# Out-projection by seven products over all eight token tiles, with its right blocks and those of FFN pair 1 prepared in stage one through GpSimd's DMA queue

## The chip, the cores and the metric

One core of a Trainium2 chip runs the whole layer. The time is that of the device in microseconds, the median of several executions of the same program. TensorE (PE in the profile, with PEld for its weight loads) multiplies. VectorE (DVE), ScalarE (ACT) and GpSimd (POOL) work on tiles in the on-chip memory SBUF and on the results in PSUM. SyncE (SP) issues DMAs in the kernel before; in the changed one GpSimd issues some too.

## The reference

One layer of a streaming encoder, on 1024 tokens of width 1024 in float32. What bears on the change is the end of the mixer and the start of the FFN:

```python
h = x @ w_in[l]
...
y_a = chunk_band_attention(heads_a(qa), heads_a(ka), heads_a(va), rel_bias[l]) @ w_proj_a[l]
y_b = stick_breaking_attention(heads_b(qb), heads_b(kb), heads_b(vb)) @ w_proj_b[l]
gate_a = jax.nn.sigmoid(ga + b_gate[l, :D])
gate_b = jax.nn.sigmoid(gb + b_gate[l, D:])
mix = (gate_a * y_a + gate_b * y_b) @ w_out[l]
x = layer_norm(DEEPNORM_ALPHA * x + mix, ln1_g[l], ln1_b[l])
gu = x @ w_ffn_in[l]
g, u = jnp.split(gu, 2, axis=-1)
ffn = (jax.nn.silu(g) * u) @ w_ffn_out[l]
x = layer_norm(DEEPNORM_ALPHA * x + ffn, ln2_g[l], ln2_b[l])
```

## The kernel before

**Numbers in two parts.** A float32 operand is split (`split`, lines 108 to 110) into a high part, a rounded copy that ScalarE casts, and a low part, which VectorE subtracts. A product of two operands is three matmuls of 128x128 by 128x512: high by high, high by low, low by high. All three add into one PSUM bank.

**Seven products.** Where a matrix product is cut into 2 x 2 blocks, seven block products of sums and differences take the place of eight (a scheme of Strassen's kind). The products have numbers 1 to 7 and run in an order such as 1, 2, 5, 3, 6, 7, 4. Two PSUM banks per tile suffice: `x`, on which products 1, 6, 7 and 4 build, and `y`, with 2 and 3 or 5 and others. The sums are made ahead, by VectorE.

**Stages.** Stage one is the input projection. Its columns are taken in pairs of blocks (`project`, `pair_steps`), each by seven products, and after the products p1, p2, p6, p5, p7, p3, p4 of a pair the PSUM banks (`sxp`, `syp`, `szp` in the profile) are copied or added into tiles `c`, which then go to DRAM (`q_dr`, `k_dr`, `g_dr`). Beside this main work stage one does side work, called from `aside_work` (line 500): `sum_wo` loads blocks of the out-projection's weights, forms four differences and stores them raw in `wt_dr`; `store_proj` loads 8 blocks of the attention's projection weights, splits them and stores both parts in `wp_dr`. Side tiles and `c` tiles share the slots of `QKV`, that is of the tags `qs`, `kh`, `kl` and `v`, with two slots each. `cycle` hands them out in turn, and who gets a slot waits until its former tile has been read for the last time, by a store for example. Every DMA is issued on SP's queue (`dma = nc.sync.dma_start`).

Then come attention with its stick-breaking part, the projection of its result, the gates, and the out-projection.

**The out-projection before** (lines 1355 to 1420) treats the token tiles 0 to 3 by seven products over two tiles at a time, and the token tiles 4 to 7 in full: eight block products each, for two halves of the columns. The seven products read `wt_drt` (stage one's differences), loaded and split on the spot by `begin_wo`. `take_in` adds a finished bank into the residual tile `acc`. `norm_1` is LayerNorm 1: statistics, aggregate, a power on POOL, and two scalings by VectorE (`L1188` and `L1191`). As soon as four token tiles are normed, `x1_operands` transposes them on TensorE (`x1ps`), copies and splits them into the FFN's operands `x1A`.

**The FFN** takes the 22 column blocks of its input weights as 11 pairs. Pair 0 is computed in full (`plain_half`, tiles `plainhl` and `plainhr`), since its operands are not summed yet. Pairs 1 to 10 go by seven products. For each, `left_f` and `right_f` load the weights `wLf` and `wRf` and form and split the sums `taf`, `tbf`. For pair 1 this happens during the out-projection.

**Order.** The tile framework's scheduler orders each engine's instructions from the program's order, and `tc.keep_in_program_order` or `tc.issue_after` pin some. An engine works its own list in order: a waiting instruction holds up all behind it, DMA issues in a queue included.

```python
QKV = ("qs", "kh", "kl", "v")
SLOTS = dict(bw=9, pt=4, yt=3, qs=2, kh=2, kl=2, v=2, gt=3, kp=4, op=8, xt=16)
```

Of the kernel before, what the change touches and what calls it, by code (L numbers as in the profile page):

```python
# [18 lines left out]
P = 128  # L19
# [29 lines left out]
def hybrid_trunk_kernel(ctx: ExitStack, tc, x, xt, w_first, w_v, w_in, b_gate, rel_bias, w_proj,  # L49
# [117 lines left out]
    def product(acc, W, ops, p, first):  # L167

        if p == 3:
# [367 lines left out]
    def begin_w(srcs, name, raw, hl, lo_eng, in_turn=False):  # L537
        r = raw(f"wr_{name}")
        srcs = srcs if isinstance(srcs, list) else [(slice(0, 1024), srcs)]
        for cs, src in srcs:  # L540
            ins = dma(r[:, cs], src)
            if in_turn:
                tc.keep_in_program_order(ins)
# [23 lines left out]
    wt_dr = {n: dram(f"wt_dr{n}_", 2) for n in ("t1", "t2", "t3", "t4")}  # L567
    wo_src = {n: [w_out[b, j] for j in range(2)] for b, n in enumerate(("11", "12", "21", "22"))}

    def sum_wo(j):  # L570

        put, sub = nc.vector.tensor_tensor, ALU.subtract
        x_, y_, z_, u_ = (cycle(QKV, f"wo{n}r{j}") for n in ("11", "12", "21", "22"))
        for t, n in ((x_, "11"), (y_, "12"), (u_, "22"), (z_, "21")):
            dma(t, wo_src[n][j])
        put(x_, y_, x_, sub)
        put(y_, u_, y_, sub)
        put(u_, u_, x_, sub)
        put(z_, z_, u_, sub)
        for t, n in ((x_, "t1"), (y_, "t3"), (u_, "t2"), (z_, "t4")):  # L580
            dma(wt_dr[n][j], t)
# [3 lines left out]
    def store_proj(i):  # L585
# [4 lines left out]
        for d, t in zip(wp_dr[i], load_w(srcs, f"proj{i}", take, take, nc.vector)):  # L590
            dma(d, t.bitcast(F32))
# [70 lines left out]
    def right_or_v(i):  # L662
# [3 lines left out]
        else:  # L666
# [4 lines left out]
              right_or_v, first=3, then=rest_of_start, also=aside_work, wide=V_AT - 1, then_right=2)  # L671
# [325 lines left out]
    wo = {}  # L997

    def begin_wo(name, raws, tag):
        ends = [begin_w((wt_dr if name in wt_dr else wo_src)[name][j], f"o{name}_{j}", of(raw),  # L1000
                        of(tag), nc.vector, True) for j, raw in enumerate(raws)]

        def end():
            wo[name] = [end_j(True) for end_j in ends]
        return end

    def wo_op(name, kt):
        cs = (LO, HI)[kt % 2]
        return tuple(t[:, cs] for t in wo[name][kt // 2])

# [9 lines left out]
    for si, (hd, g, st, box) in enumerate(vsteps):  # L1020
# [5 lines left out]
        if pos == 4:  # L1026
            if hidx < 15:
                load_v(heads[hidx + 1])
            else:
                next_w = begin_proj(1, 3)()  # L1030
                end_11, end_21 = (begin_wo(name, raws, "xt")
                                  for name, raws in (("11", ("qs", "kh")), ("21", ("kl", "v"))))
        if hidx == 15 and pos == 10:
            end_11()
# [49 lines left out]
    m_high = [None] * 8  # L1084
    raw_22 = slot("pt", "m22")
    m_first = [slot(tag, f"m1_{kt}", F32R) for kt, tag in enumerate(("yt", "yt", "yt", "pt"))]
    m_ab = [[None] * 4 for _ in range(2)]
    acc_t = []

    def quarter(q):  # L1090
        return slice(q * 2 * P, (q + 1) * 2 * P)

    def m_sums(kt, a, b):

        put, sub = nc.vector.tensor_tensor, ALU.subtract
        g, (q0, q1, q2, q3) = m_first[kt], (quarter(q) for q in range(4))
        split(g[:, q2], g[:, q3], b[:, q0])
        nc.scalar.copy(raw_22[:, quarter(kt)], b[:, q1])
        put(b[:, q1], a[:, q1], b[:, q1], ALU.add)
        put(a[:, q1], a[:, q0], a[:, q1], sub)  # L1100
        put(a[:, q0], b[:, q1], a[:, q0], sub)
        put(b[:, q0], b[:, q0], a[:, q0], sub)
        for n, t in enumerate((a, b)):
            o = m_ab[n][kt] = slot("bw", f"m{'ab'[n]}_{kt}", F32R)
            split(o[:, LO], o[:, HI], t[:, LO])
# [6 lines left out]
    def m_op(p, kt):  # L1112
        if p in (1, 2):
            q = 0 if p == 1 else 2
            return m_first[kt][:, quarter(q)], m_first[kt][:, quarter(q + 1)]
        if p == 4:
            return tuple(t[:, quarter(kt)] for t in ops_22)
        o, q = {6: (m_ab[0], 0), 7: (m_ab[0], 1), 3: (m_ab[1], 0), 5: (m_ab[1], 1)}[p]
        return o[kt][:, quarter(q)], o[kt][:, quarter(q + 2)]

    m_raw = {}

    def high(c):
        t = m_high[c] = cycle(QKV, f"mo{c}", F32R)
        split(t[:, LO], t[:, HI], m_raw[c][:, HI])

    for n, c in enumerate((6, 7, 5, 4, 2, 3, 1, 0)):
        if n % 2 == 0:
            w = next_w
            if n < 6:  # L1130
                next_w = begin_proj(1, (2, 1, 0)[n // 2])()
# [16 lines left out]
        if c < 4:  # L1148
            m_sums(c, m_raw[c + 4], mA)
            if n > 4:  # L1150
                high(last_c)
            last_c = c
        else:
            g = m_first[c - 4]
            split(g[:, quarter(0)], g[:, quarter(1)], mA[:, quarter(0)])
            high(c)
        if n == 0:
            end_21()
        elif n == 3:
            more_acc("pt")  # L1160
            more_acc("pt")
        elif n == 6:
            end_t2 = begin_wo("t2", ("gt", "gt"), "op")
    end_t2()
    end_t1 = begin_wo("t1", ("gt", "bw"), "op")
    end_t3 = begin_wo("t3", ("gt", "gt"), "op")
    ops_22 = [slot("xt", f"m22{q}", F32R) for q in "hl"]
    split(*ops_22, raw_22)
    more_acc("pt")
# [6 lines left out]
    def layer_norm(t, g, b, name, quick, done=lambda cs: None, n_st=2, cuts=(LO, HI),  # L1176
                   late_low=False):
        st = sml.tile([P, 24], F32, name=f"bn_{name}", tag="bn")
        mv = sml.tile([P, 3], F32, name=f"mv_{name}", tag="mv")
        w = D // n_st  # L1180
        for j in range(n_st):
            at = (j + late_low * n_st // 2) % n_st * w
            nc.vector.bn_stats(st[:, 6 * j:6 * j + 6], t[:, at:at + w])
            if j == 0:
                nc.vector.tensor_scalar(st[:, 2:3], st[:, 2:3], EPS * D, None, ALU.add)
        nc.vector.bn_aggr(mv[:, 0:2], st[:, 0:6 * n_st])
        nc.gpsimd.tensor_tensor(mv[:, 2:3], mv[:, 1:2], neghalf, ALU.pow)
        nc.vector.scalar_tensor_tensor(t, t, mv[:, 0:1], g, ALU.subtract, ALU.mult)  # L1188
        if quick:
            for cs in cuts:  # L1190
                nc.vector.scalar_tensor_tensor(t[:, cs], t[:, cs], mv[:, 2:3], b[:, cs],  # L1191
                                               ALU.mult, ALU.add)
                done(cs)
        else:
            nc.scalar.activation(t, t, AF.Copy, scale=mv[:, 2:3])
            nc.gpsimd.tensor_tensor(t, t, b, ALU.add)
# [442 lines left out]
```

## Time and profile before

| | before |
|---|---|
| median of 3 runs | 1412.49 us (1411.85 to 1413.65) |
| the profiled execution | 1412.51 us |
| its span in the trace | 1410.7 us |
| instructions on TensorE | 6642 matmuls and transposes |
| bytes moved by DMA | 292.28 MB, 207 GB/s on average |
| granted clock of TensorE | 0.999 |

The span runs from the first to the last instruction that the trace shows; 1.8 us of the execution lie around it. Matmuls are pipelined: a 128x512 matmul is shown with a length of 0.39 us, and the next starts before it ends, so the spacing of starts tells its cost. Lines in the profile are those of the kernel before. A split has the lines 109 (ScalarE) and 110 (VectorE), and most products of stage one and the FFN line 179, so groups are told apart by tile names. On the timeline stage one lies between 0 and 315 us, attention with the gates and projections from there to about 640, the out-projection from 681.5 to 766.5, and the FFN behind it.

### The profile page before, as it was taken

Reading aid. Unit: us, or ns where it says so; the run is one execution under the profiler, and the core shown is the slowest. Engines: PE = TensorE matmul, PEld = TensorE weight load, DVE = VectorE, ACT = ScalarE, POOL = GpSimd, SP = SyncE. Lnnn points to the kernel's source line nnn. Section 1 sums busy time; section 2 is a strip of 40 time slices with the busy share of each in tenths; the row PEclk is TensorE's granted clock in tenths of the full one; section 3 lists DMA queues with packets and bytes.
Section 4 is the critical chain, followed back from the end, with each engine's and each line's share of the span. In section 5 each row is a group of like instructions: output and inputs, shape, how many; then the busy total and the mean of one; then the engine's idle time right before and its main releaser. Section 6 shows DMA issues by size and latency. Waiting matters only on the chain.

```text
span 1410.7 us, 18935 instructions
## 1 busy us (share of the span) xinstructions
PE 1399.7 (99%) x6642; PEld 1164.6 (83%) x6642; DVE 1034.1 (73%) x1671; ACT 699.0 (50%) x1245; POOL 236.0 (17%) x308
## 2 busy tenths in 40 slices
PE   9999999999999999999999999999999999999997
PEld 7888888888888888888888888888888888888886
DVE  8967657545887788878998967767677765847666
ACT  6544444545888888774413644434444443322220
POOL 0000000002555878750001000000000000000033
PEclk9999999999999999999999999999999999999999
DMA  7476468856676478755651144433444349996652
GB/s 254 165 286 224 178 236 303 295 179 238 212 231 208 130 252 281 253 198 194 231 202 75 61 148 166 149 141 143 164 164 149 143 144 342 411 385 236 233 194 90
DMA packets 98927, 292.28 MB, mean 207 GB/s; under 512 B 9728, under 2 KB 26112, under 8 KB 98832
## 3 DMA queue, kind: packets, MB, share of 16 engines
q1 hardware_dynamic: 98832, 291.07, 58.2%
q8 instruction: 52, 0.85, 0.3%
q14 instruction: 43, 0.35, 0.1%
HBM read 187.20 MB, written 100.17 MB: 204 GB/s over the span
## 4 chain that ended last, share of the span: by engine, by line
PE 94%; DVE 2%; DMA 1%; ACT 1%; issue 1%; POOL 0%; DVEq 0%; SPq 0%; ACTq 0%; POOLq 0%
PE sxf L179 16%; PE d L1512 15%; PE sxp L179 9%; PE szf L179 8%; PE v L481 5%; PE gps L606 4%; PE szp L179 4%; PE syf L179 4%; PE yAps L910 3%; PE ops L1369 3%; PE syp L179 2%; PE tp_b L817 2%; PE tp_a L817 2%; PE plain L347 1%; PE pv_b L833 1%; PE pv_b L832 1%
## 5 line engine op out<-in xcount | busy, mean ns | idle before, releaser
L1512 PE MATMUL d<-wd,sl 128*128 128x512 f32 (+1 forms) x924 | 207.7, 387 | 0.0
L1512 PEld LDWEIGHTS d<-wd,sl 128*128 128x128 f32 x924 | 172.3, 188 | 35.4
L1532 POOL TENSOR_TENSOR mv<-mv,neghalf 128x1 f32<-128x1 f32 x8 | 9.0, 1121 | 606.7 <-DVE mv L1531 606.7
L109 ACT CAST wd<-wd 128x512 fp32r<-128x512 f32 x77 | 45.9, 621 | 114.1 <-PE d L1512 66.8
L794 POOL TENSOR_TENSOR w_b<-w_b,kp_b 128x511 f32<-128x511 f32 (+3 forms) x96 | 96.0, 1012 | 23.2 <-DVE kp_b L789 16.7
L110 DVE TENSOR_TENSOR sl<-h,sl 128x512 fp32r<-128x512 f32 x77 | 52.6, 686 | 27.6 <-ACT sl L109 27.6
L789 DVE TENSOR_TENSOR_SCAN kp_b<-kp_b,ident_ps 128x512 f32<-128x512 f32 (+2 forms) x64 | 56.5, 885 | 21.0 <-ACT kp_b L786 20.0
L109 ACT CAST sl<-h 128x512 fp32r<-128x512 f32 x77 | 47.5, 620 | 48.1 <-PE syf L179 18.3
L1489 DVE TENSOR_TENSOR x<-d,x 128x512 f32<-128x512 f32 (+1 forms) x41 | 27.6, 675 | 47.6 <-PE d L1512 47.5
L786 ACT ACTIVATE kp_b<-sc_b 128x512 f32<-128x512 f32 (+3 forms) x96 | 48.3, 504 | 28.0 <-PE sc_b L706 23.6
L110 DVE TENSOR_TENSOR wd<-wd,wd 128x512 fp32r<-128x512 f32 x77 | 52.7, 709 | 10.7 <-ACT wd L109 10.6
L179 PE MATMUL szf<-x1S63h,wcf 128*128 128x512 f32 x168 | 55.1, 389 | 0.0
L110 DVE TENSOR_TENSOR pt_b<-tp_b,pt_b 128x512 fp32r<-128x512 f32 (+1 forms) x96 | 49.9, 544 | 6.6 <-ACT pt_b L109 5.7
L729 POOL MEMSET bias<- 64x64 f32 x2 | 0.3, 145 | 314.3 <-ACT bias L725 314.3
L109 ACT CAST pt_b<-tp_b 128x512 fp32r<-128x512 f32 (+1 forms) x96 | 46.6, 503 | 8.0 <-PE tp_b L817 7.6
L759 POOL TENSOR_SCALAR w_a<-w_a,st_a 128x640 f32<-128x640 f32 (+2 forms) x64 | 42.2, 669 | 48.0 <-PE sc_a L706 26.6
L754 ACT ACTIVATE w_a<-w_a,st_a 128x640 f32<-128x640 f32 (+2 forms) x64 | 44.7, 700 | 8.6 <-DVE st_a L748 7.5
L787 ACT ACTIVATE w_b<-sc_b 128x511 f32<-128x511 f32 (+3 forms) x96 | 48.3, 504 | 0.0
L817 PE MATMUL tp_b<-ident,w_b 128*128 128x128 f32 x288 | 47.3, 272 | 0.2
L110 DVE TENSOR_TENSOR pt_a<-tp_a,pt_a 128x512 fp32r<-128x512 f32 (+1 forms) x96 | 44.6, 486 | 3.3 <-ACT pt_a L109 2.2
L1307 ACT ACTIVATE h<-sxf 128x512 f32<-128x512 f32 x21 | 12.6, 598 | 68.2 <-PE sxf L179 68.2
L817 PEld LDWEIGHTS tp_b<-ident,w_b 128*128 128x128 f32 x288 | 36.4, 140 | 11.1 <-DVE pt_b L110 1.1
(1574 smaller groups left out, 4285.2 us busy)
## 6 DMA issues: line engine op xcount, KB each, us to landing
s_dr<-sl SPq DMA_DIRECT2D x77, 512.0 KB, 2.6
sl<-s_dr SPq DMA_DIRECT2D x77, 512.0 KB, 7.6
wLf<-in_w_ffn_in_dram SPq DMA_DIRECT2D x22, 512.0 KB, 4.3
wRf<-in_w_ffn_in_dram SPq DMA_DIRECT2D x22, 512.0 KB, 3.6
wd<-in_w_ffn_out_dram SPq DMA_DIRECT2D x22, 512.0 KB, 8.2
v_dr<-vc SPq DMA_DIRECT2D x16, 512.0 KB, 3.4
qs<-q_dr SPq DMA_DIRECT2D x16, 512.0 KB, 6.7
kh<-k_dr SPq DMA_DIRECT2D x16, 512.0 KB, 6.5
```

The source lines that it names most:

```text
L109: return (nc.scalar.copy(dst_h, src), nc.vector.tensor_tensor(dst_l, src, dst_h.bitcast(F32), ALU.subtract))
L110: nc.vector.tensor_tensor(dst_l, src, dst_h.bitcast(F32), ALU.subtract))
L179: mm(acc, lw[:, ks], rx, start=(first and kt == i == 0), stop=(kt == 3 and i == 2), skip_group_check=not first)
L481: mm(accs[j], a, b, start=(first and kt == n == 0), stop=(kt == 3 and n == 2), skip_group_check=True)
L606: mm(acc[hf], lw[:, ks], rx[k][:, (LO, HI)[hf]], start=(k == j == 0), stop=(k == KT - 1 and j == 2))
L754: nc.scalar.activation(s[:, 0:w], s[:, 0:w], AF.Exp, bias=st[:, m:m + 1], scale=-1.0, accum_out=st[:, 2:3])
L786: nc.scalar.activation(kp[:, c0:e], sc[:, 0:n], AF.Sigmoid, scale=-1.0)
L787: nc.scalar.activation(be[:, m0:e], sc[:, m0 - c0:n], AF.Sigmoid)
L789: nc.vector.tensor_tensor_scan(kp[:, 0:e], kp[:, 0:e], ident_ps()[:, 0:e], 0.0, ALU.mult, ALU.add)
L794: nc.gpsimd.tensor_tensor(be[:, m0:e], be[:, m0:e], kp[:, m0 - 1:e - 1], ALU.mult)
L817: ins = tr(tp[:, (qb - lo_q) * P:(qb - lo_q + 1) * P], wt[qb - q0][:, (kb - qb) * P:(kb - qb + 1) * P], ident)
L1512: mm(part, a, b, start=(fresh and i == k == 0), stop=(i == n - 1 and k == 2), skip_group_check=not fresh)
```

## The change

1. The out-projection goes by seven products over all eight token tiles: product p runs over four tile positions j, so that positions j and j + 4 are the two token blocks. The order is 1, 2, 5, 3, 6, then 7 and 4 interleaved. The left-hand operands of products 3 to 7 are split one by one between the products (`m_split`, `m_sums`, `m_sums_3`).
2. Of the out-projection's right blocks, 1, 2, 3 and 5 are loaded raw and split on the spot (`wo_split`), and 4, 6 and 7 are split in stage one, stored in `wo_dr` and loaded ready for use. The block of product 5 is a difference that stage one stores raw (`t1_dr`).
3. FFN pair 1's seven right blocks are summed and split in stage one too (`sum_wf`), stored in `wf_dr`, and loaded by `load_f1`.
4. The side transfers of stage one (these, and those of `store_proj`) are issued from GpSimd's queue: `aside_dma = nc.gpsimd.dma_start`. The tables `WO_AT` and `PROJ_AT` say at which pair of stage one which side work starts, and `next_part` runs one part of it after each product.
5. LayerNorm 1 scales the second time on VectorE only for the token tiles 3, 6 and 7. For 0, 1, 2, 4 and 5 ScalarE scales, and a DMA on GpSimd's queue adds the bias `ln1b` in place (`accum_op`). LayerNorm 1 and 2 share `mark` and `finish` now, and VectorE's order around the out-projection is tied by `chain`.

```diff
+    WO_AT, PROJ_AT = (5, 7, 8, 9, 10), (6, 9, 10, 11)
     def aside_work(i):
         if i == 2:
             small_inputs()
-        if i in (2, 6):
-            sum_wo(i // 6)
-        if i >= len(work) - 9:
-            store_proj(i - len(work) + 9)
+        if i in PROJ_AT:
+            for j in range(2):
+                store_proj(2 * PROJ_AT.index(i) + j)
+        if i + 1 in WO_AT:
+            parts.extend((sum_wf, *(lambda kt=kt: sum_wo(kt) for kt in range(4)))
+                         [WO_AT.index(i + 1)]())
...
+    aside_dma = nc.gpsimd.dma_start
+    def sum_blocks(name, x_, y_, z_, u_, dst):
+        sub, put = ALU.subtract, nc.vector.tensor_tensor
+        def out(p, src, *terms):
+            def part():
+                if terms:
+                    put(src, *terms, sub)
+                if p in dst:
+                    o = cycle(("kl", "v"), f"{name}_{p}", F32R)
+                    split(o[:, LO], o[:, HI], src)
+                    aside_dma(dst[p], o.bitcast(F32))
+                elif p == 5:
+                    aside_dma(dst["t1"], src)
+            return part
+        return [out(3, u_), out(1, x_), out(5, x_, y_, x_), out(7, y_, u_, y_),
+                out(6, u_, u_, x_), out(2, z_), out(4, z_, z_, u_)]
...
+    def finish(name, n, t, g, b, lone, done, cuts=(slice(0, D),), tied=False, added=None):
...
+        nc.gpsimd.tensor_tensor(mv[:, 2:3], mv[:, 1:2], neghalf, ALU.pow)
+        for cs in cuts:
+            tie(nc.vector.scalar_tensor_tensor(t[:, cs], t[:, cs], mv[:, 0:1], g[:, cs],
+                                               ALU.subtract, ALU.mult))
+            if lone:
+                tie(nc.vector.scalar_tensor_tensor(t[:, cs], t[:, cs], mv[:, 2:3], b[:, cs],
+                                                   ALU.mult, ALU.add))
+            else:
+                nc.scalar.activation(t[:, cs], t[:, cs], AF.Copy, scale=mv[:, 2:3])
+                if added is None:
+                    nc.gpsimd.tensor_tensor(t[:, cs], t[:, cs], b[:, cs], ALU.add)
+                else:
+                    nc.gpsimd.dma_start(t[:, cs], added[:, cs], accum_op=ALU.add)
...
+    def norm_1(tt):
+        finish(f"1_{tt}", 2, acc_t[tt], g1, b1, tt == 3 or tt > 5, lambda cs: None, tied=True, added=b1)
+    def project_out(p, j):
+        accs = by if p in (2, 5, 3) else bx
+        first = p in (1, 2, 5)
...
+        for kt in range(4):
+            lh, ll = (m_ops[p][kt][:, c + j * P:c + (j + 1) * P] for c in (0, HW))
+            wh, wl = (wo[p][kt][:, cs] for cs in (LO, HI))
+            for n, (a, b) in enumerate(((lh, wh), (lh, wl), (ll, wh))):
+                mm(accs[j], a, b, start=(first and kt == n == 0), stop=(kt == 3 and n == 2),
+                   skip_group_check=not first)
+        tt, cs = j + 4 * (p in (5, 7, 4)), (LO, HI)[p in (5, 7, 3, 6)]
+        take_in(tt, cs, accs[j], 1.0 if p in (2, 6, 7) else ALPHA)
...
+    for n, (p, j) in enumerate(((7, 0), (7, 1), (4, 0), (7, 2), (4, 1), (7, 3), (4, 2), (4, 3))):
+        project_out(p, j)
+        if p == 4:
+            norm_1(j + 4)
+        if n > 3:
+            x1_operands(0, acc_t, (n - 4,))
```

Three places where the change moves instructions. The first is ScalarE in stage one, between the pairs 8 and 9 (numbers behind the tile names: `c1_8` is the first `c` tile of pair 8, `sxp8` its bank). Before:

```order
L401 COPY c1_7_1700<-sxp7_1687 128x512
L386 ACTIVATE hi1_7_1813<-c1_7_1700 128x1024
L109 CAST wbp9h_1865<-tbp9_1861 128x1024
L198 COPY c1_8_1856<-sxp8_1843 128x512
L207 COPY c2_8_1909<-sxp8_1843 128x512
```

After, the same engine one pair later, from the last copy of pair 8 to the first of pair 9:

```order
L403 COPY c1_8_1879<-sxp8_1866 128x512
L109 CAST wo0_4_1961<-wo0b_1863 128x512
L388 ACTIVATE hi1_8_2009<-c1_8_1879 128x1024
L109 CAST wcp10_2049<-wRp10_2033 128x512
L109 CAST wbp10h_2040<-tbp10_2036 128x1024
L200 COPY c1_9_2031<-sxp9_2018 128x512
```

A cast of a block of the out-projection's weights (`wo0_4`) now stands between the copies of two pairs, and its tile takes a slot of the same ring as the `c` tiles.

The second is POOL in stage one. Before, POOL's list has nothing between setting up its constants and attention; after, it holds 65 DMAs there, of which these are some (`DMA a<-b` writes a; `wo0b` and `wo1a` are raw weights, `t1_dr` and `wo_dr` the stores):

```order
L605 DMA wo0b_1863<-in_w_out_dram 128x1024
L596 DMA t1_dr0_269<-wo0a_1862 128x512
L594 DMA wo_dr7_0_277<-wo0_7_1923 128x1024
L605 DMA wo1a_2014<-in_w_out_dram 128x1024
L594 DMA wo_dr6_0_273<-wo0_6_1942 128x1024
L594 DMA wo_dr4_0_281<-wo0_4_1961 128x1024
L605 DMA wo1b_2015<-in_w_out_dram 128x1024
```

Loads and stores share one queue, so a store that waits for its split also holds up the load behind it.

The third is VectorE at the out-projection's end. The tiles `acc` are residual tiles by token tile, and `ops1_0` is a PSUM bank, which product 7 of tile 0 leaves and product 4 of tile 0 then writes. After:

```order
L1388 SCALAR_TENSOR_TENSOR acc3_7281<-acc3_7281,ops1_3_7398 128x512
L1216 BN_STATS bn1_3_7674<-acc3_7281 128x6
L1224 BN_AGGR mv1_3_7782<-bn1_3_7674 128x2
L1227 SCALAR_TENSOR_TENSOR acc3_7281<-acc3_7281,mv1_3_7782,ln1g_7332 128x1024
L1230 SCALAR_TENSOR_TENSOR acc3_7281<-acc3_7281,mv1_3_7782,ln1b_7334 128x1024
L1388 SCALAR_TENSOR_TENSOR acc4_7418<-acc4_7418,ops1_0_7336 128x512
```

And TensorE there, in groups of three matmuls, from product 7 of tile 3 to the first transposes:

```order
L1405 MATMUL ops1_3_7398<-wo7_0_7596,m7_0_7710 128x512 x3
L1405 MATMUL ops1_3_7398<-wo7_1_7597,m7_1_7713 128x512 x2
L1405 MATMUL ops1_0_7336<-wo4_0_7688,m4_0_7350 128x512 x3
L1405 MATMUL ops1_0_7336<-wo4_1_7689,m4_1_7320 128x512 x3
L1405 MATMUL ops1_0_7336<-wo4_2_7690,m4_2_7222 128x512 x3
L1405 MATMUL ops1_0_7336<-wo4_3_7691,m4_3_7267 128x512 x3
```

Before, each of these token tiles had a bank of its own per half of the columns; after, product 4 comes into a bank that VectorE must have emptied, behind the whole LayerNorm 1 of token tile 3.

More of the change, by code (lines that the diff above doesn't have):

```diff
@@ L540, in begin_w @@
         for cs, src in srcs:
-            ins = dma(r[:, cs], src)
+            ins = load(r[:, cs], src)
             if in_turn:
@@ L565, in load_w @@
         return begin_w(*args)()
[L567 to L581, printed above, removed]
+    t1_dr = [dr.tile([P, HW], F32, name=f"t1_dr{kt}") for kt in range(4)]
@@ L1081, in hybrid_trunk_kernel @@
     fill_until(1e9)
[L1084 to L1105, printed above, removed]
+    acc_t, m_raw = [], {}
+    m_ops = {p: [None] * 4 for p in range(1, 8)}
+    wo = {}
+    OUT = (1, 2, 5, 3, 6, 7, 4)
     def more_acc(tag):
@@ L1174, in bcast @@
         return t
[L1176 to L1196, printed above, removed]
-            done(slice(0, D))
+    chained = []
@@ new lines, in chain, with mark @@
+    def chain(ins):
+        for before in chained:
+            tc.add_manual_dep(ins.ins, before.ins.name, mybir.DependencyInfo(
+                mybir.DependencyClass.NoSync, mybir.DependencyReason.DATA), reason="chain")
+        chained[:] = [ins]
+        return ins
+    marks = {}
+    def mark(name, n, t, tied=False):
+        tie = chain if tied else lambda ins: ins
+        if name not in marks:
+            marks[name] = sml.tile([P, 24], F32, name=f"bn{name}", tag="bn")
+        st = marks[name]
+        tie(nc.vector.bn_stats(st[:, 6 * n:6 * n + 6], t))
+        if n == 0:
+            tie(nc.vector.tensor_scalar(st[:, 2:3], st[:, 2:3], EPS * D, None, ALU.add))
@@ new lines, in after_chain, with start_of_ffn, load_f1 @@
+    def after_chain(work):
+        with tc.issue_after(wo["last"].ins), tc.issue_after(chained[0].ins):
+            work()
+    def start_of_ffn():
+        for key, t, tag in (("hl", L0, "op"), ("hr", R0, "bw")):
+            h, l = Wf[0][key] = [slot(tag, f"wf0{key}{n}", F32R) for n in "hl"]
+            chain(split(h, l, t)[1])
+    def load_f1(ps, tag):
+        got = Wf[1].setdefault("all", {})
+        for p in ps:
+            got[p] = slot(tag, f"wf1_{p}", F32R)
+            dma(got[p].bitcast(F32), wf_dr[p - 1])
```

312 lines of the change are left out of this document (151 added, 161 removed).

## The prediction

> **What bounds the kernel now.** I read the page first (busy time and the chain that ended last), then TensorE's waits, then busy time by stretches.
>
> ```profile
> PE 1399.7 (99%) x6642; PEld 1164.6 (83%) x6642; DVE 1034.1 (73%) x1671; ACT 699.0 (50%) x1245; POOL 236.0 (17%) x308
> ...
> PE 94%; DVE 2%; DMA 1%; ACT 1%; issue 1%; POOL 0%; DVEq 0%; SPq 0%; ACTq 0%; POOLq 0%
> ```
>
> TensorE is busy in 99% of the span and makes 94% of the chain. The kernel is its instructions laid end to end, so a matmul less is worth its full spacing, and whatever makes TensorE wait costs its full length. The view of waits says how little it waits today:
>
> ```profile
> PE warm L266 <- DVE warm L263: 1.2, 1, 1.2
> PE plain L347 <- ACT xh L109: 0.4, 1, 0.4
> PE tp_a L817 <- DVE pt_a L110: 0.3, 1, 0.3
> PE plain L347 <- DVE xl L110: 0.2, 1, 0.2
> PE sxp L179 <- ACT c L198: 0.2, 1, 0.2
> ```
>
> The columns are the sum, the number and the longest. Each source waits once. The last of these rows matters below: once, TensorE waited for ScalarE's copy of a product into a tile `c`. The stretches show where the other engines have room (the first four are the end of the input projection, the fifth the end of the out-projection with LayerNorm 1):
>
> ```profile
> 175.00:210.00 35.00, 35.00 (x157) 28.96 (x156) 19.75 (x23) 16.30 (x21) 0.00 (x0) 1.00 0.63 226
> 210.00:245.00 35.00, 35.00 (x155) 28.81 (x154) 26.64 (x30) 16.72 (x21) 0.00 (x0) 1.00 0.81 303
> 245.00:280.00 35.00, 35.00 (x156) 28.99 (x155) 20.30 (x26) 19.85 (x24) 0.00 (x0) 1.00 0.83 294
> 280.00:315.00 35.00, 35.00 (x156) 29.01 (x155) 15.72 (x18) 15.53 (x19) 0.29 (x2) 1.00 0.50 182
> ...
> 740.00:760.00 20.00, 20.00 (x106) 16.89 (x105) 18.78 (x30) 11.30 (x19) 2.40 (x2) 1.00 0.15 53
> ```
>
> The columns are length, then busy time of PE, PEld, DVE, ACT and POOL, the granted clock (1.00 throughout, so the clock is no term here), the DMA share and GB/s. At 740 VectorE is 94% busy. That is where the change is tight.
>
> **The matmuls removed.** The rows of the tile `ops`, and two matmuls of it that are twelve apart:
>
> ```profile
> 650.00:800.00 150.00, 82.62 (x360) 1.00 0.45 158
> ...
> 763.78 0.39 PE L119 MATMUL ops<-wh_o,mo 128*128 128x512 f32 x1
> ...
> 766.50 0.39 PE L119 MATMUL ops<-wh_o,mo 128*128 128x512 f32 x1
> ```
>
> Twelve matmuls take 766.50 - 763.78 = 2.72 us, 0.2267 us each. Before there are 360: 7 products x 2 token tiles x 12, and 8 x 24 in full. After there are 7 x 4 x 12 = 336. So 24 x 0.2267 = **-5.44 us** if nothing waits. FFN pair 1 keeps its matmuls.
>
> **Work added to stage one (175 to 315).** The program has 20 subtractions and 19 splits of 128x512 there in place of 8 subtractions of 128x1024. Such a split's two halves, one of the wide subtractions that go, and the copy out of PSUM:
>
> ```profile
> L109 ACT CAST wcp<-wRp 128x512 fp32r<-128x512 f32 x7 | 4.4, 623 | 9.6 <-PE szp L179 9.5
> L110 DVE TENSOR_TENSOR wcp<-wRp,wcp 128x512 fp32r<-128x512 f32 x7 | 4.8, 686 | 0.1
> ...
> L576 DVE TENSOR_TENSOR wo11r<-wo12r,wo11r 128x1024 f32<-128x1024 f32 x1 | 1.2, 1226 | 1.3 <-DMA wo12r<-in_w_out_dram 1.3
> ...
> L198 ACT COPY c<-sxp 128x512 f32<-128x512 f32 x12 | 7.0, 583 | 7.4 <-DMA k_dr<-lo 3.1 <-PE sxp L179 2.2 <-DMA q_dr<-c 2.1
> ```
>
> VectorE gets 39 x 0.69 = 26.9 us less 8 x 1.23 = 9.8: +17 on 82.4 busy of 140. ScalarE gets 19 x 0.62 = 11.8 on 68.4. DMA gains 7.5 MB (12 stores of 512 KB and 4 of 256 KB in place of 8 of 512 KB; 2 loads and 7 stores for pair 1), 54 GB/s over the 140 us, on shares of 0.50 to 0.83. As throughput all of it lies beside TensorE's 140 us and costs 0. If that cover were gone, the 17 us would show in full.
>
> Latency is another matter. The last row says that ScalarE's copies out of PSUM already stood 3.1 + 2.1 us for stores (`k_dr`, `q_dr`) to free tiles, because the `c` tiles share the ring qs, kh, kl, v (two slots each) with side tiles. After, more side tiles pass through it, and their stores stand in POOL's queue. The tightest place that I find: the split `wo0_4` may start when the copy of `sxp8` is done, its store must land before `c1_9` can be written, and pair 9's product 6, which adds into the bank `sxp9`, needs that copy. Between the last matmul of `sxp8` and that product lie 33 matmuls, 33 x 0.2267 = 7.48 us. From it go 0.42 (matmul start to take, 766.50 to 766.92 below), 0.58 (copy), 0.62, 0.69 and 0.58 (copy): 4.6 us remain for issue and landing. What stores took in SP's queue in this stretch, with two loads as the slow end:
>
> ```profile
> wp_dr<-wh_proj SPq DMA_DIRECT2D x8, 512.0 KB, 2.6
> ...
> wLp<-in_w_in_dram SPq DMA_DIRECT2D x5, 512.0 KB, 6.4
> ...
> wt_drt<-wo11r SPq DMA_DIRECT2D x1, 512.0 KB, 2.9
> ...
> wt_drt<-wo12r SPq DMA_DIRECT2D x1, 512.0 KB, 4.7
> ```
>
> No DMA that POOL issues is in the trace of before. Bounded by these rows: at 2.6 nothing waits, at 4.7 such a place stalls 0.1, at 6.4 it stalls 1.8. I take 4.7, the same kind of tile in the same stretch, at about three places: **+0.3 us**, bounds 0 and 9 (five places of 1.8).
>
> The Trainium skill, "DMA: Bandwidth & Descriptors", section "Anatomy of one DMA — SWDGE (gpsimd) path", fits 2.0 us plus the bytes over 436 GB/s to such a transfer; for 512 KB that is an estimate of 3.2 us, below the 4.6 left, and the term would be 0. Against it stands the Trainium skill, "SBUF — State Buffer", section "SBUF: two separate sides": GpSimd cannot write descriptors while VectorE runs a 2-port copy, and the transfer then starts late. VectorE's rows here are tensor_tensor and scalar_tensor_tensor, and no run here shows whether they hold the descriptors up; if they did, the sum would go toward the third rival.
>
> **The out-projection's end.** After, LayerNorm 1 of eight token tiles, 28 splits of the inner operand and the transposes share the last 30 us. VectorE's rows of before give the durations; the first row is two splits back to back, the second eight transposes, with the matmul after them two rows below; the last two are the power on POOL, quick and slow:
>
> ```profile
> 754.45 1.29 DVE L110 TENSOR_TENSOR x1A<-x1raw,x1A 128x512 fp32r<-128x512 f32 x2
> ...
> 754.92 1.03 PE L1209 MATMUL x1ps<-ident,acc 128*128 128x128 f32 x8
> ...
> 755.65 0.15 DVE L1185 TENSOR_SCALAR bn<-bn 128x1 f32<-128x1 f32 x1
> ...
> 755.71 0.48 PE L116 MATMUL ops<-wh_o,mo 128*128 128x512 f32 x1
> ...
> 766.92 0.69 DVE L1348 SCALAR_TENSOR_TENSOR acc<-acc,ops 128x512 f32<-128x512 f32 x1 [0.73 <-PE ops L119]
> 767.65 0.69 DVE L1183 BATCH_NORM_STATS2 bn<-acc 128x6 f32<-128x512 f32 x1
> 768.37 0.21 DVE L1186 BATCH_NORM_AGGREGATE mv<-bn 128x2 f32<-128x12 f32 x1
> 768.62 1.28 DVE L1188 SCALAR_TENSOR_TENSOR acc<-acc,mv,ln1g 128x1024 f32<-128x1024 f32 x1
> 770.34 1.28 DVE L1191 SCALAR_TENSOR_TENSOR acc<-acc,mv,ln1b 128x1024 f32<-128x1024 f32 x1 [0.44 <-POOL mv L1187]
> ...
> 751.13 0.82 POOL L1187 TENSOR_TENSOR mv<-mv,neghalf 128x1 f32<-128x1 f32 x1 [23.35 <-DVE mv L1186]
> ...
> 768.73 1.58 POOL L1187 TENSOR_TENSOR mv<-mv,neghalf 128x1 f32<-128x1 f32 x1 [3.86 <-DVE mv L1186]
> ```
>
> Spacings: take 0.73, statistics 0.72, constant 0.15, aggregate 0.25, first to second scaling 1.72 where the second waits for the power, a scaling 1.28 or about 1.2 before unrelated work, a split of 512 columns 0.6 in a row (1.29 for two, less 0.69), of 1024 about 1.14. Set t = 0 where TensorE ends product 3 of tile 3. Unhindered, it runs product 6 (48 matmuls, 10.88), 7 of tiles 0, 1, 2 (8.16) and five matmuls of the next (1.13), and would start product 4 of tile 0 at 20.2. That product writes the PSUM bank that product 7 of tile 0 leaves, so VectorE's take of the latter comes first. VectorE's row to there, from 0.42: take, statistics, a constant and one split of tile 3, two weight splits of 1024 (0.73 + 0.72 + 0.15 + 0.6 + 2.28 = 4.5); tiles 0 and 1 with take, statistics, two splits, aggregate, scaling (4.1 each); tile 2 without splits (2.9); tile 3 with both scalings (4.7). Sum 20.3, take at 20.7, done at 21.4: TensorE waits **1.2 us**.
>
> From there to the split of the fourth transposed tile VectorE has 8 takes, 8 statistics, 4 constants, 4 aggregates, 4 first scalings (two of them waiting for the power), 2 second ones and 7 splits: 5.8 + 5.8 + 0.6 + 1.0 + 5.8 + 2.6 + 4.2 = 25.8, with 0.6 idle in it while product 4 of tile 0 ends. It is ready at 47.1. Unhindered TensorE needs it at 20.2 + 4 x 2.72 (product 4 of four tiles) + 1.6 (seven matmuls) + 4 x 0.79 (eight transposes each, 755.71 - 754.92) + 35 x 0.2267 = 43.7. So TensorE is late 3.4 us in all, the 1.2 included. With the quick power the two waits shrink by up to 0.76 each, which makes 1.9. I take **+2.9 us**, bounds 1.2 and 5 (the upper one if POOL's power for tile 3 also stands behind the accumulating transfer of tile 2, which must wait for ScalarE's scaling of 1024 columns, about twice 0.58, and that lateness stays in every later step). Behind it VectorE catches up: pair 1's three splits of 1024 and five operations of 512 (3 x 1.23 + 5 x 0.69 = 7.1 us) are gone from there.
>
> **The accumulating transfers.** LayerNorm 1's addition of its bias goes by DMA (POOL's queue) for tiles 0, 1, 2, 4, 5. Tile 2's is issued near 17.3 (scaled at 16.2, plus ScalarE) and needed by the first transposes at about 26.8: 9.5 us. By the nearest rows, a store and a load of 512 KB one after the other,
>
> ```profile
> s_dr<-sl SPq DMA_DIRECT2D x77, 512.0 KB, 2.6
> sl<-s_dr SPq DMA_DIRECT2D x77, 512.0 KB, 7.6
> ```
>
> it takes 2.6 to 10.2, so 0 to 0.7, and more only if the issue itself is late. I take 0.
>
> **Sum**, against the profiled execution: its 1412.51 are a span of 1410.7 and 1.8 around it, and it stands within 0.02 of the median 1412.49. -5.44 + 2.9 + 0.3 = -2.2: **1410.3 us**.
>
> **Rivals.**
> 1. *Clean.* The power is quick and VectorE keeps ahead: -5.44 + 0 to 1.0, **1407.1 to 1408.1**. For it: TensorE's rows at 740 show no wait while VectorE was 94% busy. Against: the walk above has VectorE short of time at both places.
> 2. *The accumulating transfer is late.* If tile 2's takes 12 us from issue, the transposes wait 2.5 more: -2.2 + 2.5, **1412.8**, no change. Nothing in the trace tells how long such a transfer takes.
> 3. *Slots freed late in stage one* (the slower side). POOL's stores hold the ring of `c` tiles. It decides from a landing of 4.6 us. At 6.4, five places (four column blocks of the out-projection's weights and one projection tile) of 1.8 give 9: -2.2 + 9, **1419**; at 5.7 it is **1416**. For it: the copies' 5.2 us of waiting for stores, and the one wait of TensorE for such a copy. Against: stores landed at 2.6 to 4.7.
> 4. *Seven products do not come out fewer.* Excluded by count, 336 against 360.
>
> **How the numbers follow.** About 0.2% (2.8 us) is what a measurement of this kernel can tell from no change, so faster means below 1409.7 and slower above 1415.3. The forecast (1408.3 to 1412.5) has 0.50, of which 0.22 is faster and 0.28 same; clean 0.17, faster; the late transfer 0.13, nearly all same; the slots 0.20, of which 0.17 is slower, since two places alone stay inside 0.2%. Faster 0.39, same 0.43, slower 0.18. The range leaves out the extreme end of the slots: 1407 to 1417.5.
>
> **What would show it.** Right: about 6618 matmuls in place of 6642; a wait of TensorE's `ops` for VectorE's take near 1.2 us, and of the first plain FFN matmuls for the split of `x1raw`, 1 to 2.5 us in all; none of `sxp`, `syp`, `szp` above 0.3. Wrong: waits of `sxp` or `szp` for ScalarE's `c` copies, released by POOL's stores (rival 3), or `x1ps` waiting for a DMA (rival 2), or no wait at all (rival 1). The weak points are the two durations that no row has: a store and an accumulation issued by POOL.

## The result and the profile after

The changed kernel takes 1448.78 us (median of 4 runs, 1447.13 to 1452.95) beside 1412.25 for the kernel before. The ratio is 1.026, with a 95% interval of 1.024 to 1.029. The prediction, 1410.3 with a range of 1407.0 to 1417.5, is wrong by 38.5 us, and on the side to which it gave 18%.

The page of the kernel after, the lines of busy time, of DMA queues and of the chain that ended last:

```profile
PE 1410.3 (97%) x6618; PEld 1169.1 (81%) x6618; DVE 1039.4 (72%) x1698; ACT 705.3 (49%) x1264; POOL 277.0 (19%) x378
...
q1 hardware_dynamic: 94368, 274.82, 53.3%
q0 software_dynamic: 8800, 31.46, 6.4%
...
PE 82%; DMA 6%; DVE 5%; issue 4%; ACT 2%; POOL 1%; DVEq 0%; SPq 0%; POOLq 0%; ACTq 0%
```

TensorE has the 24 instructions fewer that were counted, and yet 10.6 us more busy time (1399.7 before). The idle time rose too, from 1410.7 - 1399.7 = 11.0 us to 1447.9 - 1410.3 = 37.6. So the span's +37.2 us are +26.6 of idle time, -5.4 for the matmuls removed, and 10.6 + 5.4 = +16.0 because the remaining ones ran longer. TensorE's share of the chain falls from 94% to 82%, and that of DMA rises from 1% to 6%.

TensorE's waits after (sum, number, longest):

```profile
PE sxp L181 <- ACT c L200: 11.9, 4, 5.7
PE sxp L181 <- ACT c L209: 5.2, 3, 4.3
PE sc_a L742 <- issue: 4.3, 1, 4.3
PE sxf L181 <- ACT gt L200: 2.3, 1, 2.3
PE warm L268 <- DVE warm L265: 1.2, 1, 1.2
PE plainhl_0f L117 <- DVE x1A L110: 1.0, 2, 0.5
PE szp L181 <- ACT c L213: 0.8, 1, 0.8
PE sxf L181 <- ACT gt L1321: 0.7, 1, 0.7
PE ops L1405 <- DVE acc L1388: 0.5, 1, 0.5
```

The first, second and seventh rows, 17.9 us, are stage one: TensorE waits until ScalarE has copied a bank into a `c` tile. Before, the same wait was one of 0.2. The stretches where it happens, after (same columns as before; the clock is the column behind POOL's busy time):

```profile
210.00:245.00 35.00, 30.53 (x125) 24.41 (x124) 20.73 (x27) 13.77 (x18) 6.95 (x13) 0.90 0.69 259
245.00:280.00 35.00, 29.26 (x120) 23.57 (x119) 24.26 (x32) 16.39 (x22) 5.89 (x11) 0.90 0.84 298
280.00:315.00 35.00, 29.02 (x115) 22.84 (x114) 17.52 (x24) 14.10 (x19) 9.22 (x17) 0.90 0.68 249
```

TensorE is 83 to 87% busy at a granted clock of 0.90. Over the three stretches VectorE is as busy as before (62.5 us beside 62.7) and ScalarE less (44.3 beside 52.1): this is waiting, not work. Where the time goes by stage is read from the first start of five groups of matmuls, in us from the start of the span:

| first matmul of | before | after | both in SyncE's queue (e1) | last version (e12) |
|---|---|---|---|---|
| attention (`sc_a`) | 333.6 | 360.2 | 337.5 | 338.4 |
| out-projection (`ops`) | 681.5 | 715.4 | 687.2 | 687.7 |
| FFN (`plainhl`) | 766.7 | 796.0 | 767.6 | 768.2 |
| FFN's output (`d`) | 1193.0 | 1230.0 | 1200.4 | 1196.7 |
| end of the span | 1410.7 | 1447.9 | 1418.3 | 1414.6 |

Stage one costs 26.6 us, and attention's start another 7.3 (the wait of 4.3 and the low clock behind it). The out-projection gains 85.2 - 80.6 = 4.6. The FFN's first half loses 434.0 - 426.3 = 7.7.

How one stall comes about, from the timeline of the kernel after (start, length, engine, line, and in brackets the idle time before and what ended it):

```profile
221.84 0.54 POOL L627 DMA_DIRECT2D wp_dr<-wl_proj  x1 [4.73 <-DVE wl_proj L557]
222.65 1.13 POOL L547 DMA_DIRECT2D wr_proj<-in_w_proj_dram  x2 [0.27 <-issue]
...
231.24 1.04 ACT L556 CAST wh_proj<-wr_proj 128x1024 fp32r<-128x1024 f32 x1 [7.11 <-DMA wr_proj<-in_w_proj_dram]
...
233.62 0.58 ACT L209 COPY c<-sxp 128x512 f32<-128x512 f32 x1 [0.39 <-issue]
...
234.26 0.80 PE L181 MATMUL sxp<-s13h,wap8h 128*128 128x512 f32 x1 [4.34 <-ACT c L209]
...
235.28 0.63 PE L181 MATMUL sxp<-s13h,wap8l 128*128 128x512 f32 x1
235.71 0.63 PE L181 MATMUL sxp<-s13h,wap8h 128*128 128x512 f32 x1
```

GpSimd issues the store of a projection block after waiting 4.73 us for its split, and only then the next block's load. The load lands some 8 us later. ScalarE stands 7.11 us for it, since its cast comes next in its list, and the copy of the bank `sxp` stands behind the cast. TensorE waits 4.34 us for that copy, and afterwards its matmuls start 0.43 us apart, in place of 0.2267, until 238.7. Every row here happened; which of its links decides is what the experiments ask.

### The profile page after: what moved, and what is told of

Its sections match the earlier page's. It is cut to its first block, busy times and chain, and to the rows that moved or that the text cites. A ratio compares the mean times of both kernels' runs of the same rounds, so it can differ in the third digit from the quotient of the medians.

```text
span 1447.9 us, 19074 instructions
## 1 busy us (share of the span) xinstructions
PE 1410.3 (97%) x6618; PEld 1169.1 (81%) x6618; DVE 1039.4 (72%) x1698; ACT 705.3 (49%) x1264; POOL 277.0 (19%) x378
## 4 chain that ended last, share of the span: by engine, by line
PE 82%; DMA 6%; DVE 5%; issue 4%; ACT 2%; POOL 1%; DVEq 0%; SPq 0%; POOLq 0%; ACTq 0%
PE sxf L181 15%; PE d L1564 14%; PE szf L181 8%; PE sxp L181 5%; PE v L483 5%; PE gps L642 4%; PE syf L181 4%; PE ops L1405 3%; PE yAps L947 3%; PE tp_b L854 2%; PE szp L181 2%; PE tp_a L854 2%; PE plain L349 2%; DMA wr_proj<-in_w_proj_dram 1%; PE pv_b L870 1%
## 5 line engine op out<-in xcount | busy, mean ns | idle before, releaser
L1225 POOL TENSOR_TENSOR mv<-mv,neghalf 128x1 f32<-128x1 f32 x16 | 18.3, 1144 | 732.0 <-DVE mv L1224 731.9
L1405 PE MATMUL ops<-wo,m 128*128 128x512 f32 x336 | 77.5, 391 | 0.5 <-DVE acc L1388 0.5
L1405 PEld LDWEIGHTS ops<-wo,m 128*128 128x128 f32 x336 | 62.8, 188 | 13.9 <-DVE acc L1388 1.0
L109 ACT CAST pt_a<-tp_a 128x512 fp32r<-128x512 f32 (+1 forms) x96 | 39.4, 431 | 18.0 <-PE tp_a L854 17.3
```

What stands on the lines that cost most here:

```text
L109: return (nc.scalar.copy(dst_h, src), nc.vector.tensor_tensor(dst_l, src, dst_h.bitcast(F32), ALU.subtract))
L1405: mm(accs[j], a, b, start=(first and kt == n == 0), stop=(kt == 3 and n == 2), skip_group_check=not first)
```

## The experiments

Theory Q, formed from that timeline: loads stand behind stores in GpSimd's list and come late. Rivals: the added work itself (W), late landings of what GpSimd issues (S, L).

**e1: side transfers in SyncE's queue.**

```diff
-    aside_dma = nc.gpsimd.dma_start
+    aside_dma = dma
```

> The changed kernel, with the side transfers of stage one in SyncE's queue as before. Theory Q (the side loads stand behind stores in GpSimd's list, are issued late, and ScalarE, which waits for them in order, holds the copies out of PSUM back): the waits of sxp and szp in stage one fall from 18 us to under 3 and with them the low clock; 1410 to 1418 us. Theory W (the added work and the added tiles in the ring are too much, whatever the queue): the waits stay above 10 us and the time above 1430.

Measured: 1420.54 us, ratio 1.0055 (1.004 to 1.007). That one line is worth 28 us, so the queue makes most of the loss and W, which put the time above 1430, does not. The waits of `sxp` sum to 3.1 us, a little over the 3 expected, and the time is 2.5 us above the range. The rest, 8 us, remains with the work.

**e2: the kernel before, with its own side transfers in GpSimd's queue.**

```diff
-            dma(t, wo_src[n][j])
+            nc.gpsimd.dma_start(t, wo_src[n][j])
...
-            dma(wt_dr[n][j], t)
+            nc.gpsimd.dma_start(wt_dr[n][j], t)
```

and likewise the loads and stores of `store_proj`.

> The kernel before, with its own side transfers (16 loads and 16 stores of the projection weights, 8 loads and 8 stores of the out-projection's) in GpSimd's queue and no other edit. Theory Q: waits of sxp and szp for ScalarE appear, 5 to 20 us with the low clock, 1420 to 1440 us. Theory W: as before within 3 us, 1410 to 1415.

Measured: 1436.4 us, ratio 1.016 (1.0145 to 1.018), with these rows among TensorE's waits:

```profile
PE sxp L179 <- ACT c L198: 9.0, 2, 6.4
PE sxp L179 <- ACT c L207: 6.8, 1, 6.8
```

Without any new work or new tile, the move alone costs 24 us. That is inside Q's range, and W's 1410 to 1415 is excluded.

**e3 and e4: only the stores, or only the loads, left in GpSimd's queue.** In e3 `halves` and `store_proj` load by `dma`; in e4 the stores go by `dma`.

> The changed kernel, side loads in SyncE's queue, side stores left in GpSimd's. Theory Q: near the run with both in SyncE's queue, at most 4 us above it. Rival S (the stores that GpSimd issues land late, and free the slots late): within 8 us of the changed kernel's 1448.

> The changed kernel, side stores in SyncE's queue, side loads left in GpSimd's. Theory Q: the loads no longer stand behind stores that wait for a split, only behind loads that wait for a slot, so most of the loss goes: 1412 to 1425. Rival S: near the run with both in SyncE's queue as well. Rival L (loads that GpSimd issues are slow by themselves): above 1435.

Measured: e3 1442.19 us, e4 1434.89. Theory Q falls here: with all loads out of GpSimd's list 6.6 us of the 28 are won, where it asked for 24 or more, and e4 lies 10 us above its range. Rival S has e3 inside its 8 us, but e4 should then be near e1, and is 14 us above it. Rival L misses its 1435 in e4 by 0.1 us, and e3, where no load is left with GpSimd, should then be fast. The two edits win 6.6 and 13.9 us each alone, and 28.2 together (e1). By the median GpSimd's stores land little later in the kernel after than the same stores did in SyncE's queue before: `wp_dr<-wh_proj` 3.0 us beside 2.6, `wp_dr<-wl_proj` 4.3 beside 3.5.

**e5 and e6: who does the cast.** GpSimd casts and subtracts the projection blocks, with the queue of the change (e5) and with SyncE's (e6).

```diff
...
+        nc.gpsimd.tensor_copy(hi, r)
+        nc.gpsimd.tensor_tensor(lo, r, hi.bitcast(F32), ALU.subtract)
...
```

> The changed kernel, all side transfers still in GpSimd's queue, but the projection blocks' cast and subtraction done by GpSimd in place of ScalarE and VectorE. Theory A (TensorE waits because ScalarE stands in order for a side load with the copies out of PSUM behind it): ScalarE's 18 us of waiting for wr_proj are gone, the waits of sxp and szp fall from 18 us to 2 to 8, and 1448 becomes 1418 to 1432. Rival B (tiles of the ring come free late because GpSimd issues late, whoever splits): the waits stay above 14 us, 1440 or more, since GpSimd's casts make its issues later still.

> Both edits: transfers in SyncE's queue and the projection blocks split by GpSimd. Theory A: the stage-one waits of 3.1 us that the run with SyncE's queue left fall below 1.5, 1415 to 1419 beside its 1420.5. Rival B: no change, 1419 to 1423, or slower as the ring's slots are held longer by the slower engine.

Measured: e5 1444.26, e6 1426.91 us. In both it came out as rival B said: e5 is above 1440, and e6 is 6.4 us slower than e1. In e5 ScalarE's waits for `wr_proj` are gone and TensorE waits as long as ever:

```profile
PE sxp L181 <- ACT c L200: 11.9, 3, 5.8
PE sxp L181 <- ACT c L209: 7.0, 2, 4.1
```

Now ScalarE's copies stand for transfers that should free a tile (from the view of ScalarE's waits between 175 and 370):

```profile
ACT c L200 <- DMA wo_dr<-wo: 7.7, 1, 7.7
...
ACT c L209 <- DMA q_dr<-hi: 6.8, 1, 6.8
ACT c L200 <- DMA wp_dr<-wl_proj: 6.7, 2, 4.1
```

So theory A falls as well: ScalarE's order only decides which late transfer TensorE pays for. One of these, `q_dr<-hi`, is a store of the main path, issued by SyncE. That led to theory C: two queues that are busy at once delay each other's transfers.

**e8 and e9: idle copies added to the kernel before.** Eighteen copies of 512 KB, DRAM to DRAM, for which nobody waits and which hold no SBUF tile, in GpSimd's queue (e8) or in SyncE's (e9).

```diff
+    def extra(i, ins, srcs):
+        if 5 < i < 12:
+            for src in srcs:
+                spare.append(dr.tile([P, 1032], F32, name=f"spare{len(spare)}")[:, 0:1024])
+                nc.gpsimd.dma_start(spare[-1], src)
...
```

> The kernel before, all its transfers untouched in SyncE's queue, with 18 idle copies of 512 KB (DRAM to DRAM, no SBUF tile held, nobody waits for them) added in GpSimd's queue in stage one, each behind the store whose data it copies. Theory C (two queues that are full at once share the DMA engines, so that the main path's own stores of q, k and g land later, and with them the tiles of the ring come free): the stores q_dr, k_dr, g_dr take 4 us or more in place of 2.6 to 4.0, TensorE waits for ScalarE's c copies, 1416 to 1430. Rival B2 (only the side tiles, held by GpSimd's late issues, matter): no new wait, 1411 to 1414.

> The kernel before with 18 idle copies of the same size in SyncE's queue, each right behind the same store. Theory C: in one queue the stores ahead are not slowed, only what is issued behind; the main stores stay at 2.6 to 4.5 us and the time within 5 us of before. A rival of bytes alone (the added traffic slows the stores, whatever the queue): as slow as the copies in GpSimd's queue, within 3 us.

Measured: e8 1435.87 us, ratio 1.016 (1.014 to 1.018); e9 1420.45, ratio 1.0057 (1.004 to 1.007). The same number of copies costs 24 us in a second queue and 8 us in the first, which excludes both B2 and bytes alone. Both times lie above theory C's ranges, 1416 to 1430 and 5 us. And it named the wrong transfers: the main path's stores were to lengthen in e8 and not in e9, and it was the other way round (3.6, 3.5 and 3.2 us in e8, 7.3, 4.6 and 3.7 in e9, in the table below). What came late in e8 were loads and side stores. The DMA issues of the stretch 195 to 335 in e8:

```profile
wp_dr<-wl_proj SPq DMA_DIRECT2D x7, 512.0 KB, 6.0
...
wLp<-in_w_in_dram SPq DMA_DIRECT2D x4, 512.0 KB, 9.7
```

Before, `wLp` takes 6.4 in that stretch and `wp_dr<-wl_proj` 3.5. What ScalarE then waits for are the loads of the projection weights. Its rows in the same stretch, before, in e8 and in e9:

```profile
ACT wh_proj L550 <- DMA wr_proj<-in_w_proj_dram: 5.6, 5, 2.0
...
ACT wh_proj L562 <- DMA wr_proj<-in_w_proj_dram: 18.5, 5, 7.7
...
ACT wh_proj L563 <- DMA wr_proj<-in_w_proj_dram: 1.6, 2, 1.3
```

In e9 the same cast stands another 5.3 us for something that the trace doesn't show. A caution: e8 copies what was just stored, and e9 copies an input, since a copy in SyncE's queue that waits for a store would hold up the queue.

**e11: the same copies in ScalarE's queue**, each behind ScalarE's pass over the tile.

```diff
...
+                with tc.issue_after(ins.ins):
+                    nc.scalar.dma_start(spare[-1], w_in[len(spare) % 24])
...
```

> The kernel before with the same 18 idle copies of 512 KB, now in ScalarE's DMA queue, each behind ScalarE's pass over the tile that is stored. Theory C1 (any second queue that is busy beside SyncE's lengthens the loads there): within 6 us of the run with the copies in GpSimd's queue (1436), loads of wLp above 8 us. Theory C2 (GpSimd's queue alone does it, by its descriptors): near the run with the copies in SyncE's queue, 1416 to 1424.

Measured: 1435.38 us, ratio 1.016 (1.014 to 1.018), as slow as GpSimd's. The stretch 195 to 335 in e11:

```profile
wLp<-in_w_in_dram SPq DMA_DIRECT2D x4, 512.0 KB, 9.3
...
k_dr<-c SPq DMA_DIRECT2D x3, 512.0 KB, 8.7
q_dr<-hi SPq DMA_DIRECT2D x3, 512.0 KB, 11.1
```

It favours C1, that any second queue does it, over C2, and its copies are of an input, as in e9. It isn't clean, though: ScalarE's copies also show 15.5 us of waiting for the added transfers themselves, and TensorE's longest wait there, 10.6 us, ends with one of these. The queues side by side, from the views of the stretch 195 to 335 (medians from issue to landing) and of TensorE's waits:

| run | queues | MB moved | `q_dr<-hi` | `k_dr<-c` | `g_dr<-c` | `wLp` | TensorE waits in stage one | time |
|---|---|---|---|---|---|---|---|---|
| before | SP | 36.8 | 2.7 | 2.7 | 2.8 | 6.4 | 0.2 | 1412 |
| e1 | SP | 43.6 | 4.0 | 3.5 | 3.0 | 5.5 | 3.1 | 1421 |
| e9 | SP | 43.8 | 7.3 | 4.6 | 3.7 | 7.5 | 4.5 | 1420 |
| after | SP + POOL | 38.4 | 6.8 | 5.6 | 6.0 | 8.1 | 17.9 | 1449 |
| e2 | SP + POOL | 31.9 | 5.9 | 4.8 | 2.9 | 6.3 | 15.8 | 1436 |
| e8 | SP + POOL | 39.4 | 3.6 | 3.5 | 3.2 | 9.7 | 15.6 | 1436 |
| e11 | SP + ACT | 39.8 | 11.1 | 8.7 | 5.5 | 9.3 | 19.3 | 1435 |

With two queues TensorE waits 15.6 to 19.3 us, with one 3.1 to 4.5. The runs with two move fewer bytes up to 335 us only because they have got less far: from 195 us to the first matmul of attention e8, e9 and e11 move 46 MB alike. Which transfer comes late differs from run to run, and a store's median does not tell the cost: `q_dr<-hi` took longer in e9 than in any run with GpSimd's queue.

**e7, e10 and e12: the FFN's start**, all with SyncE's queue. e7 moves FFN pair 0's two splits from behind product 3 to behind product 5; e10 also gives eight sums to GpSimd; e12, on top of e7 alone, puts the splits of two transposed tiles between LayerNorm 1's scalings.

```diff
-        if p == 3:
+        if p == 5:
             after_chain(start_of_ffn)
```

> SyncE's queue, and FFN pair 0's two weight splits moved one product earlier on VectorE (behind product 5 of the out-projection in place of product 3), where VectorE has idle time. Theory D (VectorE is late by what it has to do from product 3 on, and the first FFN products pay for it with 3.0 us of waiting and a low clock): the wait of sxf for gt shrinks from 3.0 us to under 1.5 and its low clock goes, 1413 to 1418. Rival (the lateness comes from the transposes waiting for the last normed tile, which the splits don't touch): within 1.5 us of 1420.5.

> SyncE's queue, pair 0's weight splits early as in the run before (1417.6), and eight of the sixteen sums of 128x512 that make the FFN's operands (L1286 to L1289, row blocks 2 and 3) on GpSimd, which is idle there. They are left out of VectorE's list. Theory D (VectorE's list is what the first FFN products wait for): 8 x 0.6 = 4.8 us less on VectorE, the waits of sxf for gt (1.4 us) go, 1414.5 to 1416.5. Rival (GpSimd's slower sums put the splits of blocks 2 and 3 late instead): a new wait, 1418 or more.

> SyncE's queue, pair 0's splits early (1417.6), and on VectorE the two splits of the third and fourth transposed tiles stand between the two scalings of token tiles 6 and 7, where VectorE waits 0.45 us each for the power. Theory D (the order of VectorE's list there sets when the first FFN products may run): the wait of plainhl for the split (1.8 us) shrinks below 0.6 and its low clock goes, 1413.5 to 1416. Rival (the last normed tile, now later by 0.8 us, is what the transposes wait for): within 1 us of 1417.6.

Measured: e7 1417.61 us, e10 1425.21, e12 1416.25 (ratio to before 1.0025, 1.0016 to 1.0035). e7 confirms theory D in sign: 2.3 us less for VectorE behind product 3 is worth 2.9 us, and the wait of `sxf` falls from 3.0 to 1.4, while that of `plainhl` for the split rises from 1.0 to 1.8. e12 halves the latter to 0.9, which is less than was expected, and lies 0.25 us above its range. In e10 the rival came true: GpSimd's sums are late, and the FFN's first products wait for their splits.

```profile
PE szf L181 <- ACT x1S75h L109: 2.1, 1, 2.1
...
PE szf L181 <- DVE x1S75l L110: 1.5, 2, 0.9
```

No version beats the kernel before. e12 is the best with the seven products, 3.5 us above it by the medians of its own comparison (1416.25 and 1412.74).

## Why the prediction was wrong

**The matmuls removed** (-5.44): right. 336 are there, and from the first of them to the FFN the stage is shorter by 4.6 us after and 4.8 in e1, with 0.5 us of waiting in it.

**Work added to stage one**: as throughput it is hidden, as said, but not wholly. With one queue, e1 and e12 reach attention 3.9 and 4.8 us later than before, with 3 to 4 us of waits. e1 moves 43.6 MB in the stretch, as e9 does, whose idle copies make attention 7.6 us late; so the added bytes alone could account for it, which no run shows.

**The latency term** (+0.3, bounds 0 and 9) is the step that failed. It followed one store of GpSimd's, with 4.6 us to land in, and took rows of SyncE's queue, with no second one beside it, as the bounds. By kind, GpSimd's stores of 512 KB did land inside that, 3.0 to 4.3 us in the median. The store at the place that the prediction named, of `wo0_4`, did not. It was issued at 248.27 and took 8.8 us, the longest of its twelve; the copy into the first `c` tile of pair 9 waited for it, and TensorE for the copy, its longest wait of the run:

```profile
248.27 0.53 POOL L594 DMA_DIRECT2D wo_dr<-wo  x1 [2.36 <-DVE wo L110]
...
257.18 0.58 ACT L200 COPY c<-sxp 128x512 f32<-128x512 f32 x1 [5.83 <-DMA wo_dr<-wo]
...
257.81 0.79 PE L181 MATMUL sxp<-s24h,wbp9h 128*128 128x512 f32 x1 [5.74 <-ACT c L200]
...
DMA to landing us min/median/max: 2.9/3.3/8.8
```

It was not alone: the transfers issued between 245.3 and 252 us whose landing the trace shows took 6.8 to 11.1 us, SyncE's as well as GpSimd's. What the step left unasked is what two busy queues do to each other's transfers: in the stretch 195 to 335 the main path's `q_dr<-hi` went from 2.7 to 6.8 us and `g_dr<-c` from 2.8 to 6.0. e2 and e8 show that no new work is needed for such a loss, and e8 that no held tile is. The row that gave warning stood in the prediction: ScalarE's copies already waited 5.2 us for the stores `k_dr` and `q_dr` of that path. The fit that the prediction quoted from the Trainium skill, an estimate of 3.2 us for such a store, agrees with the median of 3.0 us of `wo_dr<-wo`, and not with the 8.8 at the place that decided. The Trainium skill's "DMA: Bandwidth & Descriptors", section "Queues, rings and completion order", says that each DMA engine goes round between the queues that have work for it, packet by packet. By that rule the main path shares the engines with a whole second queue, where in one queue it shares them only with what was issued earlier. The runs agree with the rule in total, e8 against e9 above all. That it is the cause, rather than something else that comes with a second queue, was argued and not shown.

The rival with late slots named the right engines, the copies into `c`, the ring and, with `wo0_4`, the place of the longest wait. Its price, 9 us at most, was too low for two reasons: it counted places of 1.8 us where waits of 4.3 to 5.7 came, and it left out the next term.

**The clock**: "no term here" was wrong by most of the 16.0 us that the remaining matmuls took longer. Four stretches behind long waits, three in stage one and one at the FFN's start, make 10.0 of them, counted from starts 0.43 us apart in place of 0.2267; a fifth lies at attention's start. The reading came from a kernel that never waited over 1.2 us. After a wait of 4.3 us and more in stage one the matmuls start 0.43 us apart for 4.4 to 5.2 us, as the timeline above shows.

**The out-projection's end** (+2.9): the place was right, the size half. TensorE waited 0.5 us for VectorE's take of product 7 (1.2 forecast) and 1.0, in two waits of the FFN's first matmuls, for splits of `x1A`. The sentence behind it, that VectorE catches up, was wrong. VectorE is busy for all of 820 to 830, and the FFN's first products wait 3.0 us (`sxf` for `gt`) and then run slowly. That stage loses 7.7 us in place of the gain of 7 us of VectorE's work that was to cover it. e7 supports that VectorE's list is what they wait for.

**The accumulating transfers** (0): right. No transpose waits for one; they took 7.0 us in the median, between the bounds of 2.6 and 10.2:

```profile
acc<-ln1b POOLq DMA_DIRECT2D x5, 512.0 KB, 7.0
```

In sum, of the 38.5 us missed 28.2 came from the queue (e1), with its low clock. The rest is read from e1's starts: stage one and attention are 5.7 us longer than before, where 0.3 was forecast, and the out-projection and the FFN's first half together 1.7 longer, where 2.5 shorter was forecast.

What stays open is the way in which the second queue delays the first: the two directions of transfers, loads in e8 and stores in e11, were not told apart. Nor is it shown cleanly that any second queue does it, and not GpSimd's alone.

## What to carry to other kernels

Moving side transfers to another engine's queue is not free room: here the DMA engines were already 50 to 83% busy in the stretches of stage one, the tightest place had 2 us of slack (4.6 less the 2.6 of a quick store), and the move cost 24 to 28 us. So price the rows of the transfers that stay, and the tightest place by its slowest landing and not by the median. A wait of TensorE of 4 to 6 us cost about one and a half times its length here, for the low clock behind it. A kernel that is one engine end to end has little to win from 24 matmuls and much to lose from each list that must keep step with it.

## What was not expected of the hardware

In these runs the low clock came after long waits only, apart from the kernel's start. In stage one of the kernel after, waits of 4.34, 5.74 and 4.54 us were each followed by 4.4, 4.9 and 5.2 us at 0.43 us per matmul; waits of 0.60, 0.84 and 1.23 us by none. In between it varies: 2.19 and 2.77 us in e4 and 2.91 in e5 had none, 2.10 in e6 and 2.78 in e3 had 3.8 and 4.0 us of it. The Trainium skill, "TensorE: Matmul & The Clock Gate", section "What's actually happening", puts both the idle time and the recovery at about 3.4 us, with half the clock between; the trace agrees with the half and with the order of both times, though 2.10 us of waiting sufficed in e6.

GpSimd's arithmetic took almost seven times as long where VectorE was busy. In e10 the same sum of 128x512 took 8.70 us the first time and 1.29 the second; VectorE, mostly with subtractions, was busy for all of the first and for the last 0.1 us of the second:

```profile
785.73 8.70 POOL L1287 TENSOR_TENSOR x1low<-x1low 128x512 f32<-128x512 f32 x1 [11.34 <-DVE x1A L110]
...
800.06 1.29 POOL L1287 TENSOR_TENSOR x1low<-x1low 128x512 f32<-128x512 f32 x1
```

The Trainium skill, "SBUF — State Buffer", section "Who interferes with whom", says that a VectorE instruction with two SBUF inputs contends with a GpSimd instruction that reads SBUF. The rows agree, though no run here took VectorE's work away to show it.
